# Splitting attention weights into float32r parts: the high part by a second ACT pass, the low part on DVE

## The chip, the cores and the metric

One core of a Trainium2 chip runs the whole program in one launch. The metric is the device time of an execution in microseconds (us). The engines of the core are PE (TensorE, matmuls), DVE (VectorE), ACT (ScalarE), POOL (GpSimd) and SP (SyncE, which only issues transfers).

## The reference, cut to what matters

The program is two transformer layers over 1024 tokens of width 1024, in float32. The first layer is forgetting attention with 16 heads of 64 and an MLP; the second mixes by pooling and an RWKV recurrence and ends in a mixture of 32 experts. The change lies in the attention of the first layer:

```python
q = rms_norm(q.reshape(B, S, N_HEADS, HEAD_DIM), q_g)
k = rms_norm(k.reshape(B, S, N_HEADS, HEAD_DIM), k_g)
...
logits = (jnp.einsum('bqhd,bkhd->bhqk', q_i, k).astype(jnp.float32) * scale
          + (F_i[..., :, None] - F[..., None, :]))
logits = jnp.where(k_pos[None, :] <= q_pos[:, None], logits, -jnp.inf)
p = jax.nn.softmax(logits, axis=-1).astype(v.dtype)
return jnp.einsum('bhqk,bkhd->bqhd', p, v)
```

Two places of it matter: the exponentials inside the softmax, and the sums of squares inside the two `rms_norm`.

## The kernel before, in words

**High and low parts.** PE multiplies float32r operands, which are rounded. To keep the precision of float32 the kernel splits an operand x into hi, which is x rounded to float32r, and lo = x - hi, and adds three products (hi·hi, hi·lo, lo·hi) in one PSUM bank. Making hi is a copy with rounding (on ACT, or a CAST on DVE); making lo is a subtraction of two tiles in SBUF (on DVE or POOL).

**The stage.** `fox` (L366) emits the attention stage. Several generators yield steps, and `Weave` (L306) merges them at build time into one program order by costs, gaps and bank holds written in the source; so every engine gets a fixed order of instructions, and works through it in order. The generators are `projections` (q, k and v for a pair of heads, by `product_steps` with weights that `weight` L79 splits: ACT L85, DVE L87, matmuls L112 to L114), `norms` (L467), `values` (L527), `maxima` (L547), `attention` (L579), `modulation`, and at the end `parts_of_o` and `outs`.

**norms** handles each pair of heads p and j (k first, then q), 16 times in all, in two halves th of 512 tokens. ACT squares a half (`sq`, L476), DVE casts it to float32r (`sqh`, L478), POOL subtracts (`sql`, L479), and PE sums both parts over the 64 rows of a head (L482, L483 into `pss`). ACT copies the sums out (`row`, L485), a transfer turns them, DVE makes the inverse root (L489, L492, L493 and lines 806 to 811 of `rsqrt`), two POOL transfers carry it back (L496), PE spreads it (L500), DVE scales (L501). Then `operands` (L509) makes the operands of the two heads: a burst of ACT copies (L516, L517, L524), each followed by a DVE subtraction (L525). The tiles `sq`, `sqh` and `sql` have one buffer each.

**maxima** finds the largest logit of each query: PE makes a block of logits (`mps`, L564, L566) and DVE reduces it (`mx`, L567). Their banks `sm` are two, and are shared with `pss`, `psb`, `vps` and `psm`. POOL transfers (L553, L575, L576) carry the maxima to the operands.

**attention** makes 192 tiles of weights, one for each head, half th and block st of 128 keys that the mask leaves; 96 are 512 wide, and 32 each are 384, 256 and 128 wide. In `scores` (L583) PE makes the logits in one of two `sc` banks (L589, L590, and L592 where the tile lies on the diagonal), ACT takes the exponential (`pe`, L594; two buffers), DVE casts it (`ph`, L596), and the low part `pl` (L599) is subtracted on DVE for every third block st and on POOL for the others. `ph` and `pl` have four buffers each. `weighted` (L602) multiplies a tile with v three score steps later (L609 to L611). `finish` (L615) copies the sums out on ACT (`ot`, L619), sends the denominators through memory and divides on POOL (L627), which waits for the transfer `hr`.

After the stage the MLP (L758) and the second layer follow in program order.

Of the kernel before, what the change touches and what calls it, by code (L numbers as in the profile page):

```python
# [7 lines left out]
F = mybir.dt.float32  # L8
R = mybir.dt.float32r
I32 = mybir.dt.int32  # L10
AF = mybir.ActivationFunctionType
ALU = mybir.AluOpType
# [353 lines left out]
def fox(K, a, h, xd, es):  # L366

    nc, tc = K.nc, K.tc
# [7 lines left out]
    with ExitStack() as s:  # L376
# [27 lines left out]
        nlo = cp.tile([P, KT, NH], F, name="nlo")  # L404
# [62 lines left out]
        def norms():  # L467

            for p in range(8):
                for j in (1, 0):  # L470
                    yield dict(need=(("raw", j, p, 1),))
                    raw = raws[j, p]
                    for th in range(2):
                        sq = pool.tile([P, HB], F, tag="sq", name=K.uid("sq"), bufs=1)
                        sl = pool.tile([P, HB], R, tag="sql", name=K.uid("sql"), bufs=1)
                        nc.scalar.activation(sq, raw[:, half[th]], AF.Square)  # L476
                        sh = pool.tile([P, HB], R, tag="sqh", name=K.uid("sqh"), bufs=1)
                        nc.vector.tensor_copy(sh, sq)  # L478
                        nc.gpsimd.tensor_tensor(sl, sq, sh.bitcast(F), op=ALU.subtract)  # L479
                        yield dict(cost=0.5, gap=1.94, bank="sm", hold=1.2)  # L480
                        ps = sm.tile([P, HB], F, tag="sm", name=K.uid("pss"))
                        nc.tensor.matmul(ps[:2], K.bones, sh, start=True, stop=False)  # L482
                        nc.tensor.matmul(ps[:2], K.bones, sl, start=False, stop=True)  # L483
                        row = pool.tile([2, HB], F, tag="row", name=K.uid("row"), bufs=1)
                        nc.scalar.activation(row, ps[:2], AF.Copy)  # L485
                        if th == 0:
                            c = pool.tile([P, 16], F, tag="irc", name=K.uid("irc"))
                        nc.sync.dma_start(c[64 * th:64 * th + 64], row.rearrange("e (c n) -> e c n", n=16))
                    nc.vector.tensor_scalar(c, c, 1.0 / 64, EPS, op0=ALU.mult, op1=ALU.add)  # L489
                    r = rsqrt(K, pool, c, 16, "irr")  # L490
                    rh = pool.tile([P, 2, 16], R, tag="irh", name=K.uid("irh"))
                    nc.vector.tensor_copy(rh[:, 0], r)  # L492
                    nc.vector.tensor_tensor(rh[:, 1], r, rh[:, 0].bitcast(F), op=ALU.subtract)  # L493
                    rr = pool.tile([8, HB], R, tag="sqh", name=K.uid("irb"), bufs=1)
                    for v in range(2):
                        nc.gpsimd.dma_start(rr[4 * v:4 * v + 4].rearrange("e (c n) -> e c n", n=16), rh[:, v])  # L496
                    for th in range(2):
                        yield dict(cost=0.25, gap=11.12 if th == 0 else 1.0, bank="sm", hold=1.4)
                        pb = sm.tile([P, HB], F, tag="sm", name=K.uid("psb"))
                        nc.tensor.matmul(pb, sel8[:, th], rr, start=True, stop=True)  # L500
                        nc.vector.scalar_tensor_tensor(raw[:, half[th]], raw[:, half[th]], K.gq if j == 0 else K.gk, pb, op0=ALU.mult, op1=ALU.mult)  # L501
                    for e in range(2):
                        old = ("att", 2 * p + e - NB)
                        for th in range(2):
                            yield dict(gap=0.58, need=(old,) if old[1] >= 0 else ())
                            operands(j, p, raw, e, th)
                    W.mark(("operands", p, j))
# [71 lines left out]
        def attention():  # L579

            late = []

            def scores(hd, th, st):  # L583
                i = hd % NB
                t0 = max(st * P, th * HB)
                wd = (th + 1) * HB - t0
                ps = sc.tile([P, HB], F, tag="sc", name=K.uid("sps"))
                diagonal = st * P >= th * HB
                nc.tensor.matmul(ps[:, :wd], kb[i][:, st * P:(st + 1) * P], qb[i][:, t0:t0 + wd], start=True, stop=False)  # L589
                nc.tensor.matmul(ps[:, :wd], ka[i][:, st * P:(st + 1) * P], qa[i][:, t0:t0 + wd], start=False, stop=not diagonal)  # L590
                if diagonal:
                    nc.tensor.matmul(ps[:, :P], mask, K.ident_r, start=False, stop=True)  # L592
                pe = pool.tile([P, HB], F, tag="pe", name=K.uid("pe"), bufs=2)
                nc.scalar.activation(pe[:, :wd], ps[:, :wd], AF.Exp, bias=nlo[:, st, hd:hd + 1])  # L594
                ph = pool.tile([P, HB], R, tag="ph", name=K.uid("ph"), bufs=LAG + 1)
                nc.vector.tensor_copy(ph[:, :wd], pe[:, :wd])  # L596
                pl = pool.tile([P, HB], R, tag="pl", name=K.uid("pl"), bufs=LAG + 1)
                eng = nc.vector if st % 3 == 1 else nc.gpsimd
                eng.tensor_tensor(pl[:, :wd], pe[:, :wd], ph[:, :wd].bitcast(F), op=ALU.subtract)  # L599
                late.append((hd, th, st, ph, pl, t0 - th * HB, wd))  # L600

            def weighted():  # L602
                hd, th, st, ph, pl, o0, wd = late.pop(0)
                vh, vl = vals[hd // 2]
                e, ns = hd % 2, 4 * (th + 1)
                if st == 0:
                    box["po"] = pv.tile([P, HB], F, tag="pv", name=K.uid("pv"))
                po = box["po"]
                nc.tensor.matmul(po[:66, o0:o0 + wd], vh[:, st, e], ph[:, :wd], start=st == 0, stop=False)  # L609
                nc.tensor.matmul(po[:64, o0:o0 + wd], vl[:, st, e], ph[:, :wd], start=False, stop=False)  # L610
                nc.tensor.matmul(po[:66, o0:o0 + wd], vh[:, st, e], pl[:, :wd], start=False, stop=st == ns - 1)  # L611
                if st == ns - 1:
                    finish(hd, th, po)

            def finish(hd, th, po):  # L615
                p, e = hd // 2, hd % 2
                sl = half[th]
                ot = pool.tile([66, HB], F, tag="ot", name=K.uid("ot"), bufs=2)
                nc.scalar.activation(ot, po[:66], AF.Copy)  # L619
                nc.sync.dma_start(den[hd:hd + 1, sl], ot[64:65])  # L620
                dn = pool.tile([64, 8], F, tag="dn", name=K.uid("dn"))
                nc.sync.dma_start(dn, den[hd:hd + 1, sl].rearrange("o (c n) -> (o c) n", n=8))
                nc.vector.reciprocal(dn, dn)
                nc.sync.dma_start(rden[hd:hd + 1, sl].rearrange("o (c n) -> (o c) n", n=8), dn)
                rb = hr[0:64]
                nc.sync.dma_start(rb, rden[hd:hd + 1, sl].to_broadcast([64, HB]))
                nc.gpsimd.tensor_tensor(ot[0:64], ot[0:64], rb, op=ALU.mult)  # L627
                nc.sync.dma_start(K.od[p, 64 * e:64 * e + 64, sl], ot[0:64])
                if th == 1:
                    W.mark(("att", hd))  # L630
                if e == 1:
                    W.mark(("o", p, th))
                if (hd, th) == (NH - 3, 1):
                    early.close()
                    xpool = es.enter_context(K.pool("xres", 1, side="right"))
                    for k in range(KT):
                        x1.append(xpool.tile([P, T], F, name=f"x1_{k}"))
                        nc.sync.dma_start(x1[k], xd[k])
                    W.mark("x1")

            LAG = 3
            box = {}
            turns = [(hd, th) for hd in range(NH - 2) for th in range(2)] + [(hd, th) for th in range(2) for hd in (NH - 2, NH - 1)]
            for hd, th in turns:
                for st in range(4 * (th + 1)):
                    wd = (th + 1) * HB - max(st * P, th * HB)
                    yield dict(cost=wd / 470, need=(("max", hd), ("values", hd // 2, 1)), after=7.22)
                    scores(hd, th, st)
                    if len(late) > LAG:
                        weighted()  # L650
            for _ in range(LAG):
                yield dict(cost=0.6, gap=2.0)
                weighted()
# [1323 lines left out]
```

## Time and profile before

| what | us |
|---|---|
| median of 3 runs (2743.01 to 2749.03) | 2743.7 |
| the profiled execution, its own time | 2739.69 |
| its span, first to last instruction | 2738.0 |
| attention stage, from the first projections to the last output product | 90 to 757 |
| the 192 tiles of attention weights | 176 to 746 |

How it is read: a row of a group of instructions ends with the busy time, the mean duration of one in ns, and, behind a second bar, the idle time of its engine just before them with what ended it. Idle time before an instruction is given as `[idle <-releaser]` in the timeline. PE's matmuls are pipelined, so that one that lasts 0.40 us lets the next start after 0.23 us. The granted clock of PE has two levels, 1.2 and 2.4 GHz, and is printed as a share of the higher one.

### The profile page before, as it was taken

The numbers are of one execution on the slowest core, as the hardware profiler recorded it, in microseconds if no ns is written. First come the engines' busy times: TensorE is split into PE (matmuls) and PEld (weight loads), VectorE is DVE, ScalarE is ACT, GpSimd is POOL, SyncE is SP. The second block draws the span as 40 slices with busy tenths as digits, with TensorE's granted clock in tenths as the row PEclk, the third lists the DMA queues.
The fourth block names the chain that finished last, engine by engine and source line by source line (L and its number), as shares of the span: only waits on it lengthen the run. The fifth ranks groups of instructions, "written<-read, shape, count | busy, mean of one in ns | idle before, by whom it ended". The sixth has DMA issues, their size and how long they took to land. (4 is left out here: it accounts for less than half of the span.)

```text
span 2738.0 us, 41952 instructions
## 1 busy us (share of the span) xinstructions
PE 2576.5 (94%) x15862; PEld 1976.4 (72%) x15862; DVE 1778.4 (65%) x3771; ACT 1119.0 (41%) x1850; POOL 528.1 (19%) x509
## 2 busy tenths in 40 slices
PE   7899899998989999999999999999999999699995
PEld 4667677776767888888888777767666677588882
DVE  5667777778677333333334668777777647799995
ACT  5344555445343211222123333332333222499982
POOL 3124444444330000000000011111111000122221
PEclk9999999999999999999999999999999799799997
DMA  7211222213424111111112422223224434599984
GB/s 246 76 48 48 57 62 49 60 44 94 130 80 131 46 48 50 47 50 47 47 50 62 125 63 45 55 39 53 56 47 92 107 118 146 196 377 380 395 336 197
DMA packets 377842, 301.07 MB, mean 110 GB/s; under 512 B 172790, under 2 KB 327942, under 8 KB 364326
## 3 DMA queue, kind: packets, MB, share of 16 engines
q1 hardware_dynamic: 300630, 276.46, 31.8%
q0 software_dynamic: 76896, 21.87, 3.8%
q8 instruction: 126, 2.06, 0.3%
q14 instruction: 78, 0.64, 0.1%
q10 hardware_dynamic: 112, 0.04, 0.0%
HBM read 265.92 MB, written 48.18 MB: 115 GB/s over the span
## 5 line engine op out<-in xcount | busy, mean ns | idle before, releaser
L85 ACT ACTIVATE whi<-raw 128x512 fp32r<-128x512 f32 (+2 forms) x269 | 168.3, 626 | 648.4 <-PE pout L113 285.1
L87 DVE TENSOR_TENSOR wlo<-raw,whi 128x512 fp32r<-128x512 f32 (+2 forms) x269 | 194.3, 723 | 184.5 <-ACT whi L85 178.3
L112 PE MATMUL pj<-hi,whi 128*128 128x512 f32 x736 | 303.5, 412 | 1.9 <-ACT fz L412 1.9
L114 PE MATMUL pj<-hi,wlo 128*128 128x512 f32 x736 | 298.6, 406 | 0.7 <-DVE wlo L87 0.7
L113 PE MATMUL pj<-lo,whi 128*128 128x512 f32 x736 | 296.2, 402 | 0.0
L1697 DVE TENSOR_TENSOR mlo<-mraw,mhi 128x1024 fp32r<-128x1024 f32 x192 | 226.7, 1217 | 5.7 <-ACT mhi L1696 5.1
L796 DVE SCALAR_TENSOR_TENSOR x<-pout,mod,x 128x512 f32<-128x512 f32 x128 | 96.1, 751 | 195.3 <-PE pout L114 194.8
L1696 ACT ACTIVATE mhi<-mraw 128x1024 fp32r<-128x1024 f32 x192 | 201.2, 1067 | 27.7 <-PE gu L1733 26.2
L114 PE MATMUL pout<-uh,wlo 128*128 128x512 f32 x512 | 204.5, 399 | 0.0
L113 PE MATMUL pout<-ul,whi 128*128 128x512 f32 x512 | 202.8, 396 | 0.0
L114 PE MATMUL pin<-hi,wlo 128*128 128x512 f32 x512 | 199.9, 390 | 2.6 <-DVE wlo L87 2.5
L112 PE MATMUL pout<-uh,whi 128*128 128x512 f32 x512 | 201.7, 394 | 0.0
L112 PE MATMUL pin<-hi,whi 128*128 128x512 f32 x512 | 199.7, 390 | 0.4 <-ACT whi L85 0.4
L113 PE MATMUL pin<-lo,whi 128*128 128x512 f32 x512 | 199.4, 389 | 0.0
L594 ACT ACTIVATE pe<-sps,nlo 128x512 f32<-128x512 f32 x192 | 110.2, 577 | 148.4 <-PE sps L592 58.5
L112 PEld LDWEIGHTS pj<-hi,whi 128*128 128x128 f32 x736 | 140.4, 191 | 37.2 <-issue 6.0
L599 POOL TENSOR_TENSOR pl<-pe,ph 128x512 fp32r<-128x512 f32 (+3 forms) x128 | 137.7, 1078 | 143.8 <-DVE ph L596 124.9
L114 PEld LDWEIGHTS pj<-hi,wlo 128*128 128x128 f32 x736 | 139.9, 190 | 33.7 <-DVE wlo L87 1.6
L113 PEld LDWEIGHTS pj<-lo,whi 128*128 128x128 f32 x736 | 140.4, 191 | 27.9 <-issue 2.1
L932 POOL DMA_DIRECT2D x2d<-x x8 | 4.4, 549 | 689.2 <-DVE x L796 686.1
L596 DVE CAST ph<-pe 128x512 fp32r<-128x512 f32 x192 | 95.8, 502 | 37.2 <-ACT pe L594 36.0
L113 PEld LDWEIGHTS pout<-ul,whi 128*128 128x128 f32 x512 | 96.4, 188 | 24.6
(614 smaller groups left out, 5940.5 us busy)
## 6 DMA issues: line engine op xcount, KB each, us to landing
mraw<-in_exp_gate SPq DMA_DIRECT2D x32, 1024.0 KB
mraw<-in_exp_up SPq DMA_DIRECT2D x32, 1024.0 KB
mraw<-in_exp_down SPq DMA_DIRECT2D x32, 1024.0 KB
raw<-in_w_mlp_in SPq DMA_DIRECT2D x72, 256.0 KB
adaw<-in_w_ada SPq DMA_DIRECT2D x64, 256.0 KB
raw<-in_w_mlp_out SPq DMA_DIRECT2D x64, 256.0 KB
raw<-in_fox_w_in SPq DMA_DIRECT2D x48, 256.0 KB
raw<-in_w_in SPq DMA_DIRECT2D x44, 256.0 KB
```

Of the source, the lines that this page charges most:

```text
L85: nc.scalar.activation(hi, raw, AF.Copy)
L87: nc.vector.tensor_tensor(lo, raw, hi.bitcast(F), op=ALU.subtract)
L112: mm(ps, wh, xh, start=start, stop=False)
L113: mm(ps, wh, xl, start=False, stop=False)
L114: mm(ps, wl, xh, start=False, stop=stop)
L594: nc.scalar.activation(pe[:, :wd], ps[:, :wd], AF.Exp, bias=nlo[:, st, hd:hd + 1])
L596: nc.vector.tensor_copy(ph[:, :wd], pe[:, :wd])
L599: eng.tensor_tensor(pl[:, :wd], pe[:, :wd], ph[:, :wd].bitcast(F), op=ALU.subtract)
L796: nc.vector.scalar_tensor_tensor(x[f][:, sl], ps, K.mod[:, 40 + f:41 + f], x[f][:, sl], op0=ALU.mult, op1=ALU.add)
L932: nc.gpsimd.dma_start(x2d[k], x[k])
L1696: nc.scalar.activation(view(h), src, AF.Copy)
L1697: nc.vector.tensor_tensor(view(l), src, view(h).bitcast(F), op=ALU.subtract)
```

## The change

The cast of the squares and of the exponentials on DVE goes; ACT applies the same function a second time to the same input and writes its result as float32r. All subtractions of these two places are on DVE. The first pass, to float32, stays.

```diff
@@ norms
                         nc.scalar.activation(sq, raw[:, half[th]], AF.Square)
                         sh = pool.tile([P, HB], R, tag="sqh", name=K.uid("sqh"), bufs=1)
-                        nc.vector.tensor_copy(sh, sq)
-                        nc.gpsimd.tensor_tensor(sl, sq, sh.bitcast(F), op=ALU.subtract)
+                        nc.scalar.activation(sh, raw[:, half[th]], AF.Square)
+                        nc.vector.tensor_tensor(sl, sq, sh.bitcast(F), op=ALU.subtract)
@@ attention, scores
                 nc.scalar.activation(pe[:, :wd], ps[:, :wd], AF.Exp, bias=nlo[:, st, hd:hd + 1])
                 ph = pool.tile([P, HB], R, tag="ph", name=K.uid("ph"), bufs=LAG + 1)
-                nc.vector.tensor_copy(ph[:, :wd], pe[:, :wd])
+                nc.scalar.activation(ph[:, :wd], ps[:, :wd], AF.Exp, bias=nlo[:, st, hd:hd + 1])
                 pl = pool.tile([P, HB], R, tag="pl", name=K.uid("pl"), bufs=LAG + 1)
-                eng = nc.vector if st % 3 == 1 else nc.gpsimd
-                eng.tensor_tensor(pl[:, :wd], pe[:, :wd], ph[:, :wd].bitcast(F), op=ALU.subtract)
+                nc.vector.tensor_tensor(pl[:, :wd], pe[:, :wd], ph[:, :wd].bitcast(F), op=ALU.subtract)
```

The steps that `Weave` merges, their costs and their gaps are the same, and so is the order of all other instructions.

## Rows read from the trace of the kernel before

**Rows 1.** Windows view, the attention stage: length, busy of each engine (instructions), clock, DMA.
```profile
90.00:757.00 667.00, 623.46 (x2948) 469.49 (x2949) 481.14 (x1035) 322.89 (x560) 271.11 (x269) 0.96 0.26 66
```

**Rows 2.** Waits view, engine PE, 90 to 757 us: total us, times, longest.
```profile
PE mps L564 <- DVE mx L567: 14.6, 18, 2.2
...
PE sps L589 <- ACT pe L594: 4.2, 7, 1.3
PE pss L482 <- DVE mx L567: 3.6, 5, 1.3
...
PE pss L483 <- POOL sql L479: 2.1, 3, 1.1
PE pv L611 <- POOL pl L599: 1.8, 3, 0.9
```

**Rows 3.** Lines view, 90 to 757 us; the last row keeps shapes apart.
```profile
L599 POOL TENSOR_TENSOR pl<-pe,ph 128x512 fp32r<-128x512 f32 (+3 forms) x128 | 137.7, 1078 | 143.8 <-DVE ph L596 124.9 <-DVE rsq L809 8.3 <-DVE mod L183 3.3
L594 ACT ACTIVATE pe<-sps,nlo 128x512 f32<-128x512 f32 x192 | 110.2, 577 | 148.4 <-PE sps L592 58.5 <-PE sps L590 33.0 <-POOL pl L599 28.3
...
L596 DVE CAST ph<-pe 128x512 fp32r<-128x512 f32 x192 | 95.8, 502 | 37.2 <-ACT pe L594 36.0
...
L599 DVE TENSOR_TENSOR pl<-pe,ph 128x512 fp32r<-128x512 f32 (+2 forms) x64 | 39.7, 620 | 1.6
...
L476 ACT ACTIVATE sq<-raw 128x512 f32<-128x512 f32 x32 | 20.2, 631 | 13.6 <-POOL sql L479 12.6
...
L478 DVE CAST sqh<-sq 128x512 fp32r<-128x512 f32 x32 | 15.1, 470 | 7.7 <-PE pss L482 6.8 <-ACT sq L476 0.6
...
L599 DVE TENSOR_TENSOR pl<-pe,ph 128x512 fp32r<-128x512 f32 x32 | 22.9, 715 | 0.6
```

**Rows 4.** Waits view, all engines, 90 to 757 us.
```profile
ACT pe L594 <- PE sps L592: 58.5, 33, 4.3
...
POOL ot L627 <- DMA hr<-rden: 46.6, 15, 6.9
DVE ph L596 <- ACT pe L594: 36.0, 55, 2.1
...
ACT pe L594 <- POOL pl L599: 28.3, 28, 3.0
...
ACT sq L476 <- POOL sql L479: 12.6, 9, 3.8
```

**Rows 5.** Timeline, 300 to 305 us: start, duration, engine, line, idle before.
```profile
300.67 1.29 POOL L627 TENSOR_TENSOR ot<-ot,hr 64x512 f32<-64x512 f32 x1 [6.93 <-DMA hr<-rden]
...
301.06 1.45 DVE L172 SCALAR_TENSOR_TENSOR adacc<-adaw,cact,adacc 128x512 f32<-128x512 f32 x1 [2.90 <-DMA adaw<-in_w_ada]
...
302.43 0.97 DVE L489 TENSOR_SCALAR irc<-irc 128x16 f32<-128x16 f32 x1
...
304.04 0.85 PE L564 MATMUL mps<-ka,qa 65*128 65x512 f32 x2 [1.13 <-DVE mx L567]
```

**Rows 6.** Source view, two lines on DVE: duration ns, minimum/median/maximum.
```profile
L172 DVE SCALAR_TENSOR_TENSOR adacc<-adaw,cact,adacc x56: 715/751/1776, 87.0 to 872.2; 128x512 f32<-128x512 f32 x56
L489 DVE TENSOR_SCALAR irc<-irc x16: 163/176/1936, 103.5 to 647.6; 128x16 f32<-128x16 f32 x16
```

**Rows 7.** Windows view, ten us each from 171, 241, 281, 311, 431, 511, 541, 621, 661.
```profile
sum 90.00, PE 82.71 PEld 59.12 DVE 77.06 ACT 73.06 POOL 37.76; mean PE 9.19 PEld 6.57 DVE 8.56 ACT 8.12 POOL 4.20
```

**Rows 8.** The same nine windows, line L594 alone.
```profile
sum 90.00, ACT 21.26; mean ACT 2.36
```

**Rows 9.** The same nine windows, line L476 alone.
```profile
sum 90.00, ACT 5.04; mean ACT 0.56
```

**Rows 10.** Timeline, 511 to 520 us, ACT and DVE.
```profile
514.94 0.46 ACT L594 ACTIVATE pe<-sps,nlo 128x256 f32<-128x256 f32 x1
...
515.30 0.58 ACT L619 ACTIVATE ot<-pv 66x512 f32<-66x512 f32 x1
...
519.17 0.61 DVE L567 TENSOR_REDUCE mx<-mps 128x1 f32<-128x128 f32 x2
```

## The prediction

> **What bounds the kernel now.** I read the stage first, then the waits inside it. The windows view gives the attention stage, 667 us long: PE is busy for 623.5 us of it, DVE for 481.1, ACT for 322.9 and POOL for 271.1, and the granted clock is 0.96 [rows 1]. PE is the engine whose order sets the end: it is idle for 667 - 623.5 = 43.5 us. Of the clock's two levels, 2.4 and 1.2 GHz, a mean of 0.96 means that 0.08 of the stage, 53 us, ran at the lower one; PE got through half as much there, which is 0.04 x 667 = 26.7 us. So 70 us is all that any edit of this stage could bring while PE's own work stays.
>
> Next comes who owns PE's idle time. In the waits view for PE the largest owner is DVE's maximum `mx` (14.6 us before `mps` and 3.6 us before `pss`); POOL's low parts own 2.1 and 1.8 us, ACT's exponential 4.2 us [rows 2]. That is 22.1 us for DVE and POOL together, half of PE's idle time. The rest hangs on transfers and other operands.
>
> Then why DVE is late. One stretch shows it: POOL multiplies `ot` from 300.67, and L172 on DVE beside it takes 1.45 us; L489, a tile 16 wide, takes 0.97 us, and PE stands 1.13 us before the next `mps` [rows 5]. The same lines have medians of 0.751 and 0.176 us and maxima of 1.776 and 1.936 us [rows 6]. So DVE instructions are held while POOL works, and here that alone cost DVE 0.70 + 0.79 = 1.5 us, more than PE's wait. POOL in turn is held: `ot` waits 46.6 us in all for its transfer, and the low parts queue behind it, so that ACT waits 28.3 us for a `pe` buffer and 12.6 us for `sq` [rows 4].
>
> **The change, part by part.**
>
> *DVE.* It loses 192 casts, 95.8 us, and 32 casts of squares, 15.1 us; together 110.9 us [rows 3]. It gains POOL's 128 low parts. The 64 that it does already take 0.620 us in the mean; both sets are 384 wide in the mean (by the program 64, 16, 32 and 16 tiles against 32, 16, none and 16 of 512, 384, 256 and 128), so 128 x 0.620 = 79.4 us; 32 low parts of squares at 0.715 us are 22.9 us [rows 3]. Net -8.6 us: by instruction counts DVE is hardly relieved. The relief is the contention: POOL keeps its 32 multiplications (16 heads, two halves) and its transfers, and loses 137.7 us of low parts and those of the squares.
>
> *A rule on that contention.* The trace shows DVE instructions held beside POOL's multiply [rows 5, 6]. The Trainium skill, "SBUF — State Buffer", section "Who interferes with whom", says that DVE and GpSimd share one port pair, that casts in a 2-port mode take it exclusively, and that a DVE instruction with two SBUF inputs contends with GpSimd's reads. The trace agrees as far as it goes. By that rule the change takes away the casts and most of POOL's reads, but each of the 32 multiplications left can still hold one of the 192 two-input low parts, at an estimated 0.70 us as L172 was held: 22 us of DVE time stay exposed. It enters no term below.
>
> *ACT.* It gains 192 second exponentials, 110.2 us, and 32 second squares, 20.2 us: 130.4 us [rows 3]. Neighbours overlap a little: an exponential that lasts 0.46 us from 514.94 is followed at 515.30, 0.10 us before its end [rows 10]. With 224 x 0.10 = 22 us off, ACT goes from 322.9 to about 431 us, 65% of the stage. I price the rounding output like the plain one. In the mean that is covered, since ACT runs ahead: one of its waits on PE's logits alone is 58.5 us [rows 4]. But ACT works in order and its work comes in bursts, where `operands` makes its copies. I looked for stretches of 10 us whose ACT work would not fit; there are nine. In them ACT is busy for 73.06 us, 21.26 of it exponentials and 5.04 squares [rows 7 to 9]. Twice these is 73.06 + 26.30 = 99.36 us in 90: 9.4 us too many. That is PE's loss if it can run no further ahead: the two `sc` banks are now held by two passes.
>
> *Bounds of that loss.* Below: ACT falls behind by one tile and catches up between the bursts, and nothing is lost; a gain is excluded, as work is only added. Above: nothing of the 26.3 us is absorbed. I take 9.4, nearest to what the rows force.
>
> *The waits that go.* With no low part on POOL, PE's 3.9 us on them go and ACT's 40.9 us on POOL go; what is late next for ACT is DVE's low part. Of DVE's 18.2 us with `mx`, some stay: a maximum also stands behind a low part that now waits for the second exponential, about 0.58 us later than the cast could start. The cast waits for ACT in 55 of 192 cases today [rows 4], so up to 55 x 0.58 = 32 us of DVE time comes back as idle time, and behind it queue `mx` and L525, for which PE waits. In the burst at 511 us `mx` starts at 519.17, behind such a cast [rows 10]; there the change brings nothing. Between nothing and 22.1 us I take half, 11 us, since one of my two stretches is relieved and the other not. With a quarter of PE's idle time gone (11 of 43.5) I give back a quarter of the clock's 26.7 us, 6.7 us; its ends are nothing and half, 13.4.
>
> *The rest.* The second square waits for the single `sqh` buffer as the cast did; the `row` copy ahead of it on ACT waits for the same sums, so I cost that at nothing (without that cover, 6.8 us of DVE's wait would move to ACT [rows 3]). No transfer is added or moved on SP. POOL's transfers issue earlier, as their queue is emptier; I count nothing for it. The order of PE is unchanged.
>
> **Sum:** -11 - 6.7 + 9.4 = -8.3 us. The profiled execution took 2739.69 us (span 2738.0), so 2731.4; the median of the runs is 4.0 us above it, so 2743.7 - 8.3 = 2735.4 us. About 0.2%, 5.5 us, is what a measurement of this kernel can tell from no change.
>
> **Rivals.**
>
> *ACT becomes the bound of the bursts (slower).* Place: from `norms`' squares to the last `operands` copy, nine times. The added 2.9 us each time (26.3 / 9) are not absorbed, since PE needs `sc` banks, weights and maxima that all stand behind the exponentials in ACT's or DVE's queue. It pays 26.3 us, keeps the 11 us of waits but not the clock: +15 us, 2759. It decides from the point where bursts eat more than the 17.7 us gained, two thirds of what is added. For it: the nine windows are over-full by rows. Against it: ACT's waits on POOL vanish, and four `ph` buffers and three tiles of lag remain.
>
> *Waits only change owner (same).* The low part comes where cast and low part came; `mx` starts when it did; PE's 22.1 us are the same under other names and the bursts are absorbed: 2744. For it: DVE's net load of -8.6 us and its 55 waits. Against it: stretched instructions as in [rows 5].
>
> *The whole contention was the bound (much faster).* All 22.1 us go and half of the clock's loss, against the 9.4: -22.1 - 13.4 + 9.4 = -26 us, 2718. For it: DVE's held instructions stand right before PE's waits. Against it: the burst at 511 us. The Trainium skill's "SBUF — State Buffer" ("Who interferes with whom") would make it so.
>
> That the change does not do what it says is no rival I give weight: each edit names its engine.
>
> **How the numbers follow.** Forecast 0.36, all contention 0.10, owner change 0.22, ACT-bound 0.32. So faster 0.46, same 0.22, slower 0.32; the likeliest case gives 2735.4. Its own range is 2720 to 2738. The extremes of the terms are -22.1 - 13.4 = -35.5 us with no loss in the bursts (2708) and +26.3 us with no gain (2770); leaving a tenth out at each side gives 2711 to 2764.
>
> **What would show it.** Right: two groups like L594 of 192 each at about 577 ns; no casts on DVE; POOL at about 100 us or less in the stage (271.1 - 137.7, and 32 more at about 1.08), DVE at 430 to 470 us, ACT near 431 us; L172 and L489 near their medians; PE's wait on `mx` near 9 us and its wait on ACT's exponential up from 4.2 us to about 10. Wrong on the slow side: PE's wait for the exponentials over 20 us, DVE's low part waiting for ACT more than 60 us, ACT without gaps in the nine stretches, a granted clock below 0.96. Wrong on the fast side: `mx` waits under 4 us with a clock of 0.98. A second pass that takes much longer than 0.58 us would break the ACT term itself.

## The result and the profile after

The changed kernel takes 2725.4 us in the median of 5 runs (2722.32 to 2728.06), beside 2743.7 us (2740.97 to 2750.96) for the kernel before on the same chip: 18.3 us less, a ratio of 0.993 with a 95% interval of 0.991 to 0.995. Faster, by about twice what was forecast.

The profiled execution took 2725.18 us, its span is 2723.4. The last product of weights with v starts at 739.0 us where it started at 754.4, so the 14.5 us between the two profiled executions arise in the attention stage. The stage and its waits, each fence over 90 to 757 us as before. First the windows view (columns as in [rows 1]):

```profile
90.00:757.00 667.00, 627.56 (x3013) 475.32 (x3012) 450.83 (x986) 431.38 (x794) 95.32 (x115) 0.98 0.27 69
```

ACT went from 322.89 to 431.38 us, POOL from 271.11 to 95.32, DVE from 481.14 to 450.83. PE put 65 more matmuls into the same stretch, at a clock of 0.98 where it was 0.96. The waits view of PE, which answers to [rows 2]:

```profile
PE mps L564 <- DVE mx L567: 8.6, 16, 1.4
PE sps L589 <- ACT ph L596: 7.0, 15, 1.6
PE pss L482 <- DVE mx L567: 3.1, 3, 1.3
...
PE psb L500 <- DMA irb<-irh: 2.5, 2, 1.8
...
PE sps L590 <- DMA qa<-mxd: 1.4, 1, 1.4
```

The wait for `mx` fell from 14.6 to 8.6 us, both waits on POOL are gone, and the wait on ACT before a score product rose from 4.2 to 7.0. A row that the prediction did not read fell too; before it was:

```profile
PE psb L500 <- DMA irb<-irh: 4.7, 3, 2.3
```

The lines view, which answers to [rows 3] (from L599 of the kernel before on, line numbers are one lower):

```profile
L598 DVE TENSOR_TENSOR pl<-pe,ph 128x512 fp32r<-128x512 f32 x192 | 115.9, 608 | 56.8 <-ACT ph L596 54.4 <-PE pv L610 1.0 <-PE mps L566 0.2
L594 ACT ACTIVATE pe<-sps,nlo 128x512 f32<-128x512 f32 x192 | 111.1, 578 | 75.0 <-PE sps L592 45.5 <-PE sps L590 20.2 <-DVE pl L598 3.5
L596 ACT ACTIVATE ph<-sps,nlo 128x512 fp32r<-128x512 f32 x192 | 110.5, 576 | 0.0
L172 DVE SCALAR_TENSOR_TENSOR adacc<-adaw,cact,adacc 128x512 f32<-128x512 f32 x42 | 32.9, 783 | 20.3 <-DMA adaw<-in_w_ada 20.1
L479 DVE TENSOR_TENSOR sql<-sq,sqh 128x512 fp32r<-128x512 f32 x32 | 22.6, 706 | 9.5 <-ACT sqh L478 4.6 <-PE vps L541 4.4
...
L478 ACT ACTIVATE sqh<-raw 128x512 fp32r<-128x512 f32 x32 | 20.1, 628 | 10.2 <-PE pss L482 6.4 <-PE psb L500 3.6
```

The pass that rounds costs what the plain one costs, 576 against 578 ns, and it follows without a gap. The low part of DVE takes 608 ns in the mean over all 192 (estimate: 620). In the waits view of all engines, DVE's low part now waits for the second exponential (first row), and ACT's waits of 28.3 and 12.6 us on POOL [rows 4] became waits on DVE of 3.5 and 1.6 us:

```profile
DVE pl L598 <- ACT ph L596: 54.4, 77, 2.2
...
ACT pe L594 <- DVE pl L598: 3.5, 5, 1.1
...
ACT sq L476 <- DVE sql L479: 1.6, 4, 0.8
```

The source view of the two lines of [rows 6]. DVE is still held now and then: inside the stage two of L172 took over 0.9 us and four of L489 over 0.3, and in the timeline each of the six lies beside a multiplication `ot` that POOL keeps:

```profile
L172 DVE SCALAR_TENSOR_TENSOR adacc<-adaw,cact,adacc x56: 712/751/1635, 89.4 to 856.4; 128x512 f32<-128x512 f32 x56
...
L489 DVE TENSOR_SCALAR irc<-irc x16: 159/175/1274, 105.8 to 629.6; 128x16 f32<-128x16 f32 x16
```

**Two sentences ahead of this are wrong.** The section on the change says that the order of all other instructions is the same, and the prediction says it of PE. The order in which `Weave` emits is the same. But the framework that builds the program puts each engine's instructions in a new order, by its own estimate of when each is ready, and moving work between engines moves these estimates. Of the 3,204 PE instructions that `fox` emits, 343 stand in another place in the built program; of the 955 on DVE that both kernels share 269, of the 625 on ACT 159. Score products come 3.4 places later in the mean of those that moved, `mps` 1.7 later, projections 1.5 earlier. So part of the time could come from the order, and five of the twelve experiments are about that.

### The profile page after: what moved, and what is told of

Same layout as the page of the kernel before. It is cut to its first block, busy times and chain, and to the rows that moved or that the text cites. A ratio compares the mean times of both kernels' runs of the same rounds, so it can differ in the third digit from the quotient of the medians.

```text
span 2723.4 us, 42074 instructions
## 1 busy us (share of the span) xinstructions
PE 2574.6 (95%) x15862; PEld 1978.2 (73%) x15862; DVE 1740.9 (64%) x3707; ACT 1223.1 (45%) x2074; POOL 343.6 (13%) x349
## 5 line engine op out<-in xcount | busy, mean ns | idle before, releaser
L87 DVE TENSOR_TENSOR wlo<-raw,whi 128x512 fp32r<-128x512 f32 (+2 forms) x269 | 188.7, 703 | 177.1 <-ACT whi L85 168.7
L598 DVE TENSOR_TENSOR pl<-pe,ph 128x512 fp32r<-128x512 f32 x192 | 115.9, 608 | 56.8 <-ACT ph L596 54.4
L594 ACT ACTIVATE pe<-sps,nlo 128x512 f32<-128x512 f32 x192 | 111.1, 578 | 75.0 <-PE sps L592 45.5
L114 PEld LDWEIGHTS pin<-hi,wlo 128*128 128x128 f32 x512 | 96.1, 188 | 25.4 <-DVE wlo L87 5.4
L112 PEld LDWEIGHTS pout<-uh,whi 128*128 128x128 f32 x512 | 96.1, 188 | 22.8
```

The costliest lines, as they stand in the source:

```text
L87: nc.vector.tensor_tensor(lo, raw, hi.bitcast(F), op=ALU.subtract)
L112: mm(ps, wh, xh, start=start, stop=False)
L114: mm(ps, wl, xh, start=False, stop=stop)
L598: nc.vector.tensor_tensor(pl[:, :wd], pe[:, :wd], ph[:, :wd].bitcast(F), op=ALU.subtract)
```

## The experiments

**How the runs are read.** A run gives its time, its span and the mean granted clock. As the clock has two levels, span x 2 x (1 - clock) is the length spent at 1.2 GHz, and half of that is the most that the lower level cost. The time less this half is called the time at full clock here. Its mean has a standard error of 0.4 to 1.8 us for the kernels here, and a difference of two such means one of 0.8 to 1.8. In 84 runs of the kernel before, over three sessions: 2655.5 us at full clock and 174.9 us at the lower level; in 5 of the changed kernel 2645.1 and 161.3. So of 17.2 us between the means, 10.4 are waits and other work, and 6.8 are the clock (half of 13.6). In the table each kernel stands against the kernel before on the same chip. The waits views are of one execution each.

| kernel | median us | ratio, 95% interval | at full clock | clock |
|---|---|---|---|---|
| e2: second passes alone | 2749.6 | 1.0032 (1.0016 to 1.0047) | +0.4 | +7.8 |
| e3: low parts alone | 2725.4 | 0.9930 (0.9909 to 0.9951) | -10.8 | -7.2 |
| p1: changed, old order | 2743.8 | 0.9998 (0.9984 to 1.0011) | -0.4 | +0.4 |
| p2: before, new order | 2751.0 | 1.0026 (1.0012 to 1.0040) | +4.7 | +3.9 |
| p4: low parts alone, old order | 2731.1 | 0.9967 (0.9956 to 0.9978) | -9.6 | +0.7 |
| p5: changed with copies, old order | 2741.5 | 0.9998 (0.9986 to 1.0010) | -3.1 | +2.1 |
| e5: changed with copies | 2724.6 | 0.9942 (0.9927 to 0.9958) | -12.4 | -3.8 |
| p8: changed, old order on PE alone | 2728.7 | 0.9950 (0.9934 to 0.9967) | -8.9 | -6.5 |
| p6: changed, POOL busy on `ph` | 2741.3 | 1.0005 (0.9991 to 1.0020) | -1.5 | +2.4 |
| p7: changed, POOL busy on a constant | 2739.0 | 0.9987 (0.9974 to 1.0001) | -0.7 | -4.1 |
| p9: before, three `pe` | 2743.4 | 0.9995 (0.9983 to 1.0008) | -0.4 | -0.5 |
| e6: changed, a third cast on DVE | 2721.9 | 0.9926 (0.9909 to 0.9944) | -12.8 | -9.6 |

### The two parts alone

Second passes alone (against the changed kernel):

```diff
-                        nc.vector.tensor_tensor(sl, sq, sh.bitcast(F), op=ALU.subtract)
+                        nc.gpsimd.tensor_tensor(sl, sq, sh.bitcast(F), op=ALU.subtract)
...
-                nc.vector.tensor_tensor(pl[:, :wd], pe[:, :wd], ph[:, :wd].bitcast(F), op=ALU.subtract)
+                eng = nc.vector if st % 3 == 1 else nc.gpsimd
+                eng.tensor_tensor(pl[:, :wd], pe[:, :wd], ph[:, :wd].bitcast(F), op=ALU.subtract)
```

> Only the high parts move to the second ACT pass (ACT some 431 us busy between 90 and 757, DVE some 110 less than before); the low parts stay on POOL and DVE as before. Theory A, the gain is POOL's absence: DVE's and POOL's operations still lengthen each other, ACT still waits some 28 us for POOL's low parts, and ACT is fuller by 108 us, so near the kernel before, 2734 to 2748 us. Rival C, the gain is DVE's 224 casts gone: most of the gain stays, 2724 to 2730 us.

Low parts alone (against the changed kernel):

```diff
-                        nc.scalar.activation(sh, raw[:, half[th]], AF.Square)
+                        nc.vector.tensor_copy(sh, sq)
...
-                nc.scalar.activation(ph[:, :wd], ps[:, :wd], AF.Exp, bias=nlo[:, st, hd:hd + 1])
+                nc.vector.tensor_copy(ph[:, :wd], pe[:, :wd])
```

> Only the low parts move: all on DVE, with the casts left there too; ACT is as before (323 us between 90 and 757), POOL makes none. DVE then has 451 us of the changed kernel plus 224 casts of some 0.45 us, some 550 of 667. Theory A: POOL's absence gives its gain, and a fuller DVE takes part of it back where the maxima wait: 2726 to 2742 us, faster than the kernel before and slower than the changed one. Rival C, DVE's relief is the gain: slower than before, 2748 us or more. Rival D, ACT's bursts cost the changed kernel some 9 us which this kernel does not pay: below it, 2712 to 2722 us.

The low parts alone bring all of it, 2725.4 us, just below the range of theory A and above that of rival D. The second passes alone make the kernel slower, 2749.6, above both ranges. So the 224 casts that left DVE were not the gain: e2 relieves DVE the most (385 us busy in the stage), and PE only waits elsewhere. The waits view of PE in e2:

```profile
PE sps L589 <- ACT ph L596: 10.5, 14, 1.9
PE mps L564 <- DVE mx L567: 7.9, 13, 1.2
```

In e3 DVE is fuller than before, 514.55 us in the stage against 481.14, and PE still waits less for its `mx`, 11.3 us against 18.2. The casts themselves became shorter with POOL's low parts gone: 395 ns against 502 [rows 3], 20.4 us over 192. Its lines view:

```profile
L598 DVE TENSOR_TENSOR pl<-pe,ph 128x512 fp32r<-128x512 f32 x192 | 112.3, 588 | 5.4 <-DVE ph L596 0.5
...
L596 DVE CAST ph<-pe 128x512 fp32r<-128x512 f32 x192 | 75.4, 395 | 22.5 <-ACT pe L594 21.3
```

### The order

The kernels p1, p2, p4, p5 and p8 hold the shared instructions of the stage in an order read from the other built program, by edges that order without a wait:

```diff
         W.run()
+        traced = [i for i in nc.cur_bb.bb.instructions[first:] if i.name not in extra]
...
+            row = [mine[k + m] for k, m in enumerate(moved)]
+            for one, two in zip(row, row[1:]):
+                tc.add_manual_dep(two, one.name, mybir.DependencyInfo(mybir.DependencyClass.NoSync, mybir.DependencyReason.DATA), reason="order")
```

> The changed kernel, with the instructions that both kernels share in the attention stage (3,204 on PE, 955 on DVE, 625 on ACT, 139 on POOL) held in the order in which the kernel before issues them; the new ACT passes and DVE subtractions fall in where they may. Left to itself the changed kernel has 343 of the 3,204 PE instructions in another place, 3.1 places away on average. Theory A, the engines' work (POOL no longer lengthens DVE's operations, nobody waits for POOL): the order is worth nothing, so as the changed kernel, 2723 to 2729 us. Rival B, the other order is the gain: as the kernel before, 2740 to 2747 us.

> The kernel before, with the shared instructions of the attention stage held in the order in which the changed kernel issues them. Theory A: as the kernel before, 2740 to 2747 us. Rival B: as the changed kernel, 2722 to 2730 us. If both are halfway, each has a share.

Neither: the changed kernel in the old order loses the whole gain, and the kernel before in the new order is slower than in its own. Each order suits the kernel it was made for. In p1 PE waits at the score products, for the second pass. Its waits view of PE:

```profile
PE sps L614 <- ACT ph L621: 16.6, 23, 3.0
PE mps L589 <- DVE mx L592: 7.0, 10, 2.1
PE pss L507 <- DVE mx L592: 6.8, 2, 4.0
```

> Low parts all on DVE, casts kept on DVE (the kernel of e3_low_only, 2725.4 us in its own order), with the shared instructions of the attention stage held in the order of the kernel before. Theory A, POOL's absence is the gain and needs no other order: 2721 to 2731 us. Rival B, the gain comes only together with the order that the scheduler makes for it: 2738 to 2747 us.

The low parts alone keep 9.6 of 10.8 us at full clock in the old order; what they lack there is the clock's share (2731.1 us, at the upper end of theory A). Against p4, p1 adds only the second passes: -0.4 less -9.6, 9.2 us at full clock, with a standard error of 1.2. So the second passes do cost, in this order. The traces show where: in the nine stretches that the prediction looked at. Counted on PE from the score product that starts nearest to the begin of a stretch in the kernel before to the one nearest to its end, the nine take 88.2 us before, 88.2 in p4, 99.9 in p1 and 92.3 in the changed kernel.

In the orders made for the two kernels the same step is -10.4 less -10.8, 0.4 us with a standard error of 2.3, and the medians are equal. Their two profiled executions alone say more: from the first score product to the last product with v, the changed kernel takes 565.7 us at full clock and e3 557.3 (570.3 before). So the runs show that the second passes cost far less in the built order than in the old one, and not that they cost nothing. The waits view of PE in p4:

```profile
PE mps L589 <- DVE mx L592: 12.8, 20, 1.9
PE sps L614 <- ACT pe L619: 4.3, 6, 1.9
...
PE pss L507 <- DVE mx L592: 2.7, 5, 1.0
PE psb L525 <- DMA irb<-irh: 2.5, 3, 1.7
```

Is it the score bank, which two passes now hold? The copy takes `ph` from `pe` in SBUF and lets the bank go after the first pass:

```diff
-                nc.scalar.activation(ph[:, :wd], ps[:, :wd], AF.Exp, bias=nlo[:, st, hd:hd + 1])
+                nc.scalar.activation(ph[:, :wd], pe[:, :wd], AF.Copy)
```

> The changed kernel in the order of the kernel before (2743.8 us, PE waiting 16.6 us for the second pass before a score product), but the second pass copies pe from SBUF instead of taking the exponential of the scores again, so that the score bank is free after the first pass. ACT's work stays the same. Theory E, the second pass costs by holding the bank: PE's wait falls to some 5 us and the time to 2724 to 2734 us. Rival F, it costs by filling ACT: 2739 to 2748 us.

> The same copy from SBUF in the order that the scheduler makes for it. Theory E: PE's 7.0 us of waiting for the second pass in the changed kernel go, 2717 to 2724 us. Rival F: no change against the changed kernel, 2723 to 2728 us.

Mostly not. In the old order PE's wait at the score products halves, and other waits take its place; the time stays at 2741.5, and the nine stretches take 100.2 us, as in p1. In its own order the kernel is at 2724.6, as with the second exponential; the interval does not exclude a microsecond or two. The waits view of PE in p5:

```profile
PE sps L614 <- ACT pe L619: 8.0, 13, 1.5
PE pss L507 <- ACT pe L619: 3.8, 1, 3.8
```

> The changed kernel, with the order of the kernel before on PE alone; DVE, ACT and POOL keep the order that the scheduler makes for that. With all four engines in the old order it took 2743.8 us, in its own 2725.4. Theory B1, PE's order is what matters (score products placed where the old kernel's shorter ACT chain freed their bank): 2737 to 2747 us. Rival B2, the loss came from ACT's or DVE's order: 2723 to 2732 us.

PE's old order alone costs little: 2728.7 us, and at full clock 8.9 of the 10.4 us stay, a difference within the error. Most of p1's loss came from the order on ACT, DVE or POOL: one trace of it is ACT's wait for `sql` before the next `sq`, 9.1 us in p1, 3.5 in p8 and 1.6 in the changed kernel. Which of the three engines it is was not tried.

### What POOL's low parts cost

> The changed kernel in its own order, and POOL subtracts each high part from itself in pieces of 104 columns for two of every three tiles, into a tile that nobody reads: POOL works beside DVE again, but no engine waits for what it makes. Left out of nothing; the output is the same. Theory A1, the gain is that POOL's operations no longer lengthen DVE's: DVE's maxima and subtractions lengthen again (the 512-column subtraction from 608 ns to over 640, the largest operations to over 1.5 us) and 10 us or more of the 18 are lost, 2735 to 2748 us. Rival A2, the gain is that nobody waits for POOL's queue: 2723 to 2730 us.

> The changed kernel in its own order, and POOL makes as many subtractions as in p6_pool_beside (448 pieces of at most 104 columns), but of the identity matrix from itself: they wait for no engine, no engine waits for them, and they run at once behind whatever POOL did last. The output is the same. Theory A1, POOL's mere work beside DVE and ACT is what cost the kernel before (p6_pool_beside lost 16 us with DVE's 512-column subtraction at 748 ns against 746): 2735 to 2748 us. Rival A2, p6_pool_beside lost by what its pieces held up, POOL's own queue of transfers and the buffers of the high part: 2723 to 2730 us.

```diff
                 if st % 3 != 1:
...
+                    for c in range(0, wd, 104):
+                        x = K.ident[:, :min(104, wd - c)]
+                        extra.append(tc.keep_in_program_order(nc.gpsimd.tensor_tensor(idle[:, :min(104, wd - c)], x, x, op=ALU.subtract)).ins.name)
```

(The kernel p6 has `ph` in the place of `K.ident`, and its pieces stand where their data puts them.) Two numbers of these expectations are off: the pieces are 512 and not 448, and 608 ns is the mean over all widths, where the 512-wide subtraction alone takes 746. Nobody needs what POOL makes here, and PE's order is the changed kernel's, yet 8.9 and 9.7 us at full clock of the 10.4 are lost again. DVE's part in that is small: the low part takes 611 and 640 ns against 608, and PE's waits for `mx` are 13.8 and 12.5 us against 11.7. The lines view and the waits view of PE in p7:

```profile
L630 POOL TENSOR_TENSOR idle<-ident_r 128x104 f32<-128x104 f32 (+4 forms) x512 | 237.6, 464 | 35.9
...
L625 DVE TENSOR_TENSOR pl<-pe,ph 128x512 fp32r<-128x512 f32 x192 | 122.1, 640 | 58.4 <-ACT ph L623 57.1
```
```profile
PE sps L616 <- ACT ph L623: 9.1, 15, 1.9
PE mps L591 <- DVE mx L594: 9.0, 18, 1.2
PE psb L527 <- DMA irb<-irh: 5.0, 4, 2.2
PE pss L509 <- DVE mx L594: 3.5, 3, 1.5
...
PE sps L617 <- DMA qa<-mxd: 2.8, 2, 2.4
```

Of these rows the largest rise is that of the two transfers that POOL itself issues, from 2.5 and 1.4 us to 5.0 and 2.8; in p6 `irb` stands at 6.5, and the wait for the second pass before a score product rises as much, from 7.0 to 11.3. The transfers queue behind POOL's pieces: from the end of `mrow` on DVE to the issue of `mxd` on POOL it is 0.37 us in the mean of 16 in the changed kernel, 1.00 in p6, 1.83 in p7 (and 0.59 in the kernel before, from the same rows of the timeline). So both kernels show that a busy POOL can cost the stage about as much as its low parts did, without anyone waiting for a low part. They do not separate work beside DVE from transfers issued late, as was meant: p7 delays the transfers more than the kernel before did, and neither brings back the long DVE instructions of the kernel before, which the pair at the end of this section shows.

> The kernel before in its own order, with three buffers for pe instead of two (the room comes from row, which lies in free rows of another tile), so that ACT no longer waits the 28.3 us for POOL's low parts to let go of pe. POOL works as before. Theory A2, the kernel before lost by waiting for POOL: 7 to 12 us faster than before, 2730 to 2737 us. Rival A1, POOL's work beside the others is the loss, whoever waits: within 3 us of the kernel before, 2739 to 2746 us.

```diff
+        ots = [cp.tile([P, HB], F, name=f"ots{i}") for i in range(2)]
+        rows = ots[0]
...
-                        row = pool.tile([2, HB], F, tag="row", name=K.uid("row"), bufs=1)
+                        row = rows[96:98]
...
-                pe = pool.tile([P, HB], F, tag="pe", name=K.uid("pe"), bufs=2)
+                pe = pool.tile([P, HB], F, tag="pe", name=K.uid("pe"), bufs=3)
```

ACT's 28.3 us on POOL shrink to 4.1 and the time does not move: ACT now stands before PE's logits instead, 82.7 us where it was 58.5 [rows 4]. These waits were never on the path. PE's waits in p9 stand within 1.7 us of those before, row by row, which tells how much one execution's rows can vary. ACT's waits in p9:

```profile
ACT pe L621 <- PE sps L619: 82.7, 47, 5.0
...
ACT pe L621 <- POOL pl L626: 4.1, 5, 1.4
```

What is left, from the pair in one order (before and p4): PE's waits on POOL's products go (3.9 us), those on `irb` fall from 4.7 to 2.5, those on `mx` from 18.2 to 15.5. That is 8.8 us, but waits on other owners, `psm` and `vps` among them, rose by some 4 us, so that the rows of these two executions account for 5 of the 9.6 us at full clock. DVE's own time falls by more than that, and not only in its casts: its other subtractions of two tiles in SBUF were lengthened too. The lines view, before and in p4:

```profile
L87 DVE TENSOR_TENSOR wlo<-raw,whi 128x512 fp32r<-128x512 f32 x56 | 44.1, 787 | 25.3 <-ACT whi L85 23.3 <-PE pss L483 1.4 <-DVE fe L423 0.2
...
L525 DVE TENSOR_TENSOR qb<-raw,qa 64x512 fp32r<-64x512 f32 x16 | 16.6, 1040 | 1.3 <-ACT qa L516 0.9
```
```profile
L87 DVE TENSOR_TENSOR wlo<-raw,whi 128x512 fp32r<-128x512 f32 x58 | 40.0, 692 | 15.9 <-ACT whi L85 13.9 <-PE pss L508 1.6 <-DVE fe L448 0.2
...
L550 DVE TENSOR_TENSOR qb<-raw,qa 64x512 fp32r<-64x512 f32 x16 | 10.9, 679 | 1.1 <-ACT qa L541 0.7
```

The 64 subtractions of L525 take 59.4 us before, 45.9 in p4 and 46.8 in the changed kernel; with the casts (24.5 us) and the rest, DVE's instructions other than the low parts are some 60 us shorter in p4, group by group. In p6 and p7 those 64 take 48.3 and 46.3 us: POOL's pieces, 479 and 464 ns in the mean where a low part took 1078 [rows 3], hold DVE little. How far `mx` and `irb` came later by DVE's lengthened instructions and how far by POOL's queue stays open.

### A mixture

```diff
-                nc.scalar.activation(ph[:, :wd], ps[:, :wd], AF.Exp, bias=nlo[:, st, hd:hd + 1])
+                if st % 3 == 1:
+                    nc.vector.tensor_copy(ph[:, :wd], pe[:, :wd])
+                else:
+                    nc.scalar.activation(ph[:, :wd], ps[:, :wd], AF.Exp, bias=nlo[:, st, hd:hd + 1])
```

> All low parts on DVE; the high part by the second ACT pass for two of three tiles and by DVE's cast for the third (st % 3 == 1), so that DVE stands near 480 us of 667 between 90 and 757 and ACT near 395, where the changed kernel has 451 and 431 and the one with all casts on DVE 515 and 331. Theory A: both ends measure 2725.4 us, the middle waits less on either side, 2718 to 2724 us. Rival: what waits is the chain of one tile, not the share, and it stays at 2723 to 2728 us.

2721.9 us, the lowest of all, with PE's waits for `mx` at 6.5 us and for the exponentials at 3.9. Its interval (0.9909 to 0.9944) overlaps that of the changed kernel (0.991 to 0.995), so it beats the kernel before for certain and the changed one perhaps; theory A and its rival are not told apart. The windows view:

```profile
90.00:757.00 667.00, 630.47 (x3022) 478.10 (x3021) 466.56 (x1052) 403.55 (x733) 97.67 (x116) 0.97 0.27 70
```

## Why the prediction was right, and where it was not

**Direction and range** held; 2735.4 was 10 us too high. The miss has nearly the size of one term, the charge for ACT's bursts.

- **"-11 us" of waits.** Right in size: the low parts alone are -10.8 us at full clock, -9.6 in the old order, and of the 22.1 us of rows 11.7 are left in the changed kernel. That it is half was a choice between two ends, and so partly luck. The relief that the prediction named, DVE no longer held beside POOL, is real: some 60 us of DVE's time in p4. Not all of the gain came where the prediction put it: with the order held, `mx` and POOL's products gave 6.6 us, and `irb`, 2.2 us less, stood under "POOL's transfers issue earlier ... I count nothing for it".
- **"-6.7 us" of the clock.** 6.8 measured, half of 174.9 - 161.3. That a quarter of the waits gives back a quarter of the clock was a guess, and that it fitted is luck: with p4's waits, nearly as short, no clock came back.
- **"+9.4 us" for ACT's bursts.** This term failed. The work is as priced: ACT was forecast at 431 us and stands at 431.38, a second pass at 577 ns and stands at 576. The loss is real where the order is held, 9.2 us between p4 and p1, close to the 9.4, and in the nine stretches. But the built program is ordered anew, and there the second passes cost 0.4 us by the runs' means (standard error 2.3; the two profiled executions say more). What failed is the step under it, that the old order stays. The prediction says it of PE ("The order of PE is unchanged"), but p8 keeps most of the gain with PE's old order; what counted is the order on ACT, DVE or POOL, which the section on the change took as fixed. With it fell the case of an ACT that becomes the bound of the bursts; the prediction's own lower bound, "ACT falls behind by one tile and catches up between the bursts", came nearer.
- **The waits of [rows 4].** That ACT's 40.9 us on POOL go was right; p9 shows that the 28.3 us of them at `pe` were worth nothing. They entered no term.
- **The second square.** The prediction cost its wait for the sums at nothing, since the `row` copy waits for the same sums. 6.4 us of wait did move to ACT (L478), while `row`'s own wait for them fell from 32.2 to 10.9 us. No run prices this by itself.
- **The signs.** PE's wait on ACT's exponentials 7.0 us (forecast 10), DVE's low part behind ACT 54.4 us (under 60), POOL 95.32 (100 or less), DVE 450.83 (430 to 470): all inside. PE's wait on `mx` is 8.6 us before `mps` but 11.7 with `pss` (forecast near 9). L172 and L489 came only part of the way to their medians of 751 and 175 ns, in the mean from 869 to 783 and from 524 to 358 ns.
- **The rivals.** "Waits only change owner" gives the time of p1 (2743.8 us), but there a gain of 9.6 meets a charge of 9.2, and its order was not built. "The whole contention was the bound" is nearer in its number, 2718, than the forecast is; its mechanism fell, since 12 us of PE's wait on DVE's maxima are still there.
- **DVE held beside POOL.** The casts did shorten without POOL's low parts, from 502 to 395 ns (e3) and 374 (p4), and so did the two-input subtractions of L525, from 0.93 to 0.72 us in the mean of 64 (p4); the two-input low part hardly did, 620 ns before against 608 after. The Trainium skill, "SBUF — State Buffer", section "Who interferes with whom", says that a cast in a 2-port mode contends with GpSimd, and a DVE instruction with two SBUF inputs with a GpSimd instruction that reads SBUF. The trace agrees for the casts and for L525 in the mean; for the low part p6 and p7 show 0.5% and 5%, with POOL busy over three times as long.

## What to carry to other kernels

Work on an engine that also issues transfers can cost more than its rows say: look at what queues behind it and at whose instructions it lengthens, and not only at who waits for its results. Before an unchanged order goes into a sum, compare the instructions of the built programs engine by engine, since a framework that schedules by readiness may absorb a charge that the old order would pay. A wait of an engine that runs ahead, even 28 us, can be worth nothing: ask whether its end is the end of a wait of the bounding engine.

## What was not expected of the hardware

ACT's rounding copy from SBUF is shorter than its exponential from PSUM: 522 ns in the mean of 192 (e5) against 576. And the cast on DVE had a mean of 502 ns with a maximum of 1.859 us beside POOL's low parts, while its median hardly differs from that without them (418 and 408 ns): most of the difference lies in a tail of long ones. Their source rows, before and in e3:

```profile
L596 DVE CAST ph<-pe x192: 210/418/1859, 176.8 to 745.1; 128x512 fp32r<-128x512 f32 x96, 128x384 fp32r<-128x384 f32 x32, 128x256 fp32r<-128x256 f32 x32, 128x128 fp32r<-128x128 f32 x32
```
```profile
L596 DVE CAST ph<-pe x192: 207/408/1515, 176.4 to 728.1; 128x512 fp32r<-128x512 f32 x96, 128x384 fp32r<-128x384 f32 x32, 128x256 fp32r<-128x256 f32 x32, 128x128 fp32r<-128x128 f32 x32
```
